# A decoder layer on one core: the hand-over between its parts, and w_out in blocks with sums

## The chip, the cores and the metric

One of the eight cores of a Trainium2 chip runs the whole kernel. The metric is the time in microseconds (us) that the device takes for one execution. TensorE does the matrix products and transposes, VectorE (DVE) and ScalarE (ACT) the arithmetic on tiles, GpSimd (POOL) some more of it; SyncE (SP) issues most DMAs.

## The reference

One layer for 256 tokens of 2048 features, in float32:

```
x = x + 1/2 * post1(SwiGLU_1(pre1(x)))             # FFN 1, 5632 hidden features
h = pre_mix(x);  q,k,v of two groups of 8 heads = h @ w_in
o_a = MoBA attention (one block of 256: causal softmax, partial rotary)
o_b = stick-breaking attention
x = x + post_mix(concat(norm_a(o_a), norm_b(o_b)) @ w_out)
x = x + 1/2 * post2(SwiGLU_2(pre2(x)))             # FFN 2
```

All `pre`, `post` and `norm` are RMS norms with a gain per feature. SwiGLU is `(silu(x @ w_gate) * (x @ w_up)) @ w_down`. All weights come from HBM once.

## The kernel before

**Precision.** A product of float32 is made of three matmuls on parts: every weight piece (128 x 1024 numbers) is split into a high part `whi` (a cast on ScalarE, L137) and a low part `wlo` (raw minus high, on VectorE, L142); so are the activations. The three terms are high x high, high x low, low x high. `Weights` keeps a list of pieces in the order of use, loads their blocks (up to 1 MB, three buffers, `RAW`) on SP's queue and splits three pieces ahead of the one in use (four buffers, `PARTS`). `get(i)` returns a split piece.

**Blocks with sums.** In most of the gate/up and down products, pairs of feature tiles are multiplied by the seven-product scheme for 2 x 2 blocks (two token tiles, two chunks of 512 columns): 21 matmuls instead of 24, for four sums of weights on VectorE (L104 to L110) and sums of results at the end (L913 to L924). A block holds eight PSUM banks, `1` to `7` and `X`. Plain pairs add into banks `2`, `3`, `4`, `X`. `w_out` has no such block: `products` runs it over chunks (0, 1), then 2, then 3, all plain.

**The end of a part.** The down product of an FFN ends with a tail: three pairs of feature tiles, over chunk 2 for both token tiles, then over chunk 3, token tile 0 first. From there on `ordered()` fixes the order of TensorE, VectorE, ScalarE and GpSimd as written. `handover` gives the end of the part: the last chunk of token tile 0, its RMS factor (`column`: nine small instructions of VectorE after the last sum of squares), updates of the residual `xn` (L696), the first transposes of the new `xn`; `take_over` goes on with the first three pieces of the next part, token tile by token tile, woven with the rest of the updates and transposes. GpSimd takes part: it splits halves of pieces (L142) and adds updates that ScalarE has scaled (L698, L699). The last part ends in `end_f2`, with the updates and the output DMAs.

**Small work** that need not stand at one place (`later`, `step`) is put in a list and taken up one entry a piece. SBUF beyond the weights is 30 slots of 4 KB a partition; who gives one back lets the next taker have it, in the order of giving.

Of the kernel before, what the change touches and what calls it, by code (L numbers as in the profile page):

```python
# [17 lines left out]
P = 128  # L18
# [42 lines left out]
class Weights:  # L61
# [5 lines left out]
    def __init__(self, nc, pool):  # L67
        self.nc, self.pool = nc, pool
        self.blocks, self.raw, self.pieces, self.parts = [], {}, [], {}
        self.loaded = self.split = 0  # L70

# [57 lines left out]
    def split_next(self):  # L129
# [5 lines left out]
        hi = self.pool.tile([P, nk, cols], F32R, tag="whi", name=f"whi{n}", bufs=self.PARTS)  # L135
        lo = self.pool.tile([P, nk, cols], F32R, tag="wlo", name=f"wlo{n}", bufs=self.PARTS)
# [4 lines left out]
        def low(eng, k0=0, k1=nk):  # L141
            eng.tensor_sub(lo[:, k0:k1], raw[:, k0:k1], hi[:, k0:k1].bitcast(F32))  # L142
            if then:
                then(self.raw[b])

        return low, lambda eng: low(eng, 0, nk // 2), lambda eng: low(eng, nk // 2, nk)

    def split_to(self, i):
        while self.split <= min(i, len(self.pieces) - 1):
            self.split_next()[0](self.nc.vector)  # L150
# [28 lines left out]

PLAIN = (("2", "3"), ("4", "X"))  # L180
# [9 lines left out]
H_SUMS = HALVES[0][1] + HALVES[1][1]  # L190


@with_exitstack
def hybrid_layer(ctx: ExitStack, tc: tile.TileContext, a):
# [56 lines left out]
    def plan_down(n, half, w):  # L251

        pairs, sums, tail = HALVES[half]
        for u in range(2):
            c0 = u * 2 * CH
            plan["down", n, half, u] = [
# [3 lines left out]
        if tail:  # L260
            for c in (2, 3):
                k = 2 * tail[0]
                plan["tail", n, c] = W.add(w, k, 4, c * CH, CH) + W.add(w, k + 4, 2, c * CH, CH)

    def plan_rows(w, ks):

        ks = list(ks)
        out = []
        for c0, cols in ((0, 2 * CH), (2 * CH, CH), (3 * CH, CH)):
            nk = 2048 // cols  # L270
            out.append([])
            for k in range(0, len(ks), nk):
                ids = W.add(w, ks[k], nk, c0, cols)
                out[-1] += [(k + m * nk // 2, i) for m, i in enumerate(ids)]
        return out
# [16 lines left out]
    def plan_mix():  # L292
        plan_v(1)
        plan_qk(1)
        plan_qk(0)
        plan_v(0)
        plan["o"] = plan_rows(a["w_out"], [g * NH + h for g in (1, 0) for h in range(NH)])
# [152 lines left out]
    class Pre:  # L450
# [12 lines left out]
        def update(self, c, t, eng=None):  # L463
            if self.post and (c, t) not in self.ready:
                self.post.update(c, t, eng)
# [71 lines left out]
    def product(name, pieces, x_of, done, cs, end=None):  # L537


        ps = [[bank(f"{name}_{t}{c}") for c in cs] for t in range(NT)]  # L540

        def mm(t, piece, part):
            k0 = piece[0]
            last = piece is pieces[-1]
            for j in range(part[2]):
                mm_tok(ps[t], part, j, x_of(k0 + j), t, k0 + j == 0, last and j == part[2] - 1)

        for piece in pieces[:-3] if end else pieces:
            part = W.get(piece[1])
            for t in range(NT):  # L550
                mm(t, piece, part)
            step()
        if end:
            held = [(piece, W.get(piece[1], 2 - m)) for m, piece in enumerate(pieces[-3:])]
            end([lambda t=t: done(t, cs[0], ps[t][0]) for t in range(NT)], lambda t, m: mm(t, *held[m]))
        else:
            for t in range(NT):
                for p, c in zip(ps[t], cs):
                    done(t, c, p)

    def products(name, groups, x_of, post, end):
        for m, cs in enumerate(((0, 1), (2,), (3,))):
            product(f"{name}{m}", groups[m], x_of, post.take, cs, end if m == 2 else None)

    def take_over(pre, mm, ids, need):

        after, los = pre.pending
        parts = [W.get(ids[m], 1 - m) for m in range(2)]
        if need == 4:
            his, los10 = pre.turn(1, (0,))  # L570
            run_all(his)
            _, low0, low1 = W.split_next()
            low1(nc.gpsimd)
            weave(after, los + los10)
            mm(0, parts[0], 0)
            pre.update(0, 1)
            low0(nc.vector)
        else:
            _, low0, low1 = W.split_next()
            low1(nc.gpsimd)  # L580
            weave(after[:6], los)
            mm(0, parts[0], 0)
            his, los10 = pre.turn(1, (0,))
            run_all(his)
            weave(after[6:], [lambda: low0(nc.vector)] + los10[:need])
        parts.append(W.get(ids[2], 0))
        pre.update(0, 1)
        pre.update(1, 1, nc.gpsimd)
        mm(1, parts[1], 0)
        if need == 2:  # L590
            mm(2, parts[2], 0)
            pre.post.finish(2)
        his, los = pre.turn(0, (1,))
        run_all(his)
        if need == 4:
            mm(2, parts[2], 0)
        run_all(los)
        run_all(los10[need:])
        mm(0, parts[0], 1)
        _, low0, low1 = W.split_next()  # L600
        pre.post.finish()
        low0(nc.vector)
# [757 lines left out]
```

## Time and profile before

| | us |
|---|---|
| time, median of 3 runs | 1873.37 (1873.2 to 1873.61) |
| the profiled execution, its time | 1873.02 |
| its span, first to last instruction | 1871.2 |
| TensorE matmuls busy | 1837.3 (98%) |
| VectorE busy | 1480.8 (79%) |
| ScalarE busy | 1012.3 (54%) |
| GpSimd busy | 115.4 (6%) |

The span is what the profile shows in detail; the time is the span and what lies around it. A busy TensorE can still run at half its clock, and its matmuls are drawn longer than the 0.23 us by which they follow each other. Idle time counts where the engine is needed next.

### The profile page before, as it was taken

Reading aid. Unit: us, or ns where it says so; the run is one execution under the profiler, and the core shown is the slowest. Engines: PE = TensorE matmul, PEld = TensorE weight load, DVE = VectorE, ACT = ScalarE, POOL = GpSimd, SP = SyncE. Lnnn points to the kernel's source line nnn. Section 1 sums busy time; section 2 is a strip of 40 time slices with the busy share of each in tenths; the row PEclk is TensorE's granted clock in tenths of the full one; section 3 lists DMA queues with packets and bytes.
Section 4 is the critical chain, followed back from the end, with each engine's and each line's share of the span. In section 5 each row is a group of like instructions: output and inputs, shape, how many; then the busy total and the mean of one; then the engine's idle time right before and its main releaser. Section 6 shows DMA issues by size and latency. Waiting matters only on the chain.

```text
span 1871.2 us, 23266 instructions
## 1 busy us (share of the span) xinstructions
PE 1837.3 (98%) x8638; PEld 1530.4 (82%) x8638; DVE 1480.8 (79%) x2026; ACT 1012.3 (54%) x1359; POOL 115.4 (6%) x117
## 2 busy tenths in 40 slices
PE   9999999999999998999999999999999999999997
PEld 8888888888888876888888887888888888888875
DVE  6987889778888888656786557888888778887887
ACT  7655555445555545655545446755555445555553
POOL 0000000000000002000353103000000000000001
PEclk9999999999999999999999999999999999999999
DMA  8555555455566654554445556455554555555643
GB/s 271 172 200 202 186 197 203 181 209 195 180 209 209 247 194 157 180 180 158 158 159 183 181 175 207 164 190 208 207 193 171 218 185 203 204 207 185 247 181 135
DMA packets 183121, 359.90 MB, mean 192 GB/s; under 512 B 8864, under 2 KB 58208, under 8 KB 183008
## 3 DMA queue, kind: packets, MB, share of 16 engines
q1 hardware_dynamic: 180624, 351.31, 53.8%
q0 software_dynamic: 2208, 7.04, 1.1%
q8 instruction: 68, 1.11, 0.2%
q14 instruction: 45, 0.37, 0.1%
q10 hardware_dynamic: 176, 0.07, 0.0%
HBM read 354.19 MB, written 4.19 MB: 192 GB/s over the span
## 4 chain that ended last, share of the span: by engine, by line
PE 91%; DVE 5%; ACT 1%; issue 1%; DMA 1%; POOL 0%; DVEq 0%; ACTq 0%; POOLq 0%
PE b L872 36%; PE d L872 19%; PE b_X L872 9%; PE pq L516 6%; PE pw L535 4%; PE pv L535 4%; PE d_X L872 4%; PE pq L525 3%; PE p L516 2%; DVE wlo L142 1%; PE p L525 1%; PE ht L952 1%; DVE xn L696 1%; ACT whi L137 1%; DMA raw<-in_ffn_w_gate_dram 0%
## 5 line engine op out<-in xcount | busy, mean ns | idle before, releaser
L137 ACT CAST whi<-raw 128x1024 fp32r<-128x1024 f32 (+1 forms) x793 | 790.9, 1014 | 735.4 <-PE b_X L872 301.0
L142 DVE TENSOR_TENSOR wlo<-raw,whi 128x1024 fp32r<-128x1024 f32 (+1 forms) x789 | 919.6, 1186 | 335.6 <-ACT whi L137 333.2
L872 PE MATMUL b<-whi,x 128*128 128x512 f32 x1440 | 443.9, 389 | 0.0
L872 PEld LDWEIGHTS b<-whi,x 128*128 128x128 f32 x1440 | 270.2, 188 | 56.3
L872 PE MATMUL b<-wlo,x 128*128 128x512 f32 x720 | 243.9, 389 | 0.7 <-DVE wlo L142 0.7
L872 PE MATMUL d<-whi,h 128*128 128x512 f32 x720 | 222.6, 389 | 0.4 <-ACT whi L137 0.4
L872 PE MATMUL b_X<-whi,x 128*128 128x512 f32 x480 | 186.9, 389 | 0.0
L872 PEld LDWEIGHTS b<-wlo,x 128*128 128x128 f32 x720 | 135.0, 188 | 29.6 <-DVE wlo L142 1.6
L872 PEld LDWEIGHTS d<-whi,h 128*128 128x128 f32 x720 | 135.0, 188 | 29.3 <-ACT whi L137 1.3
L516 PE MATMUL pq<-xg_mix,whi 128*128 128x512 f32 x512 | 131.8, 399 | 0.0
L872 PE MATMUL d<-wlo,h 128*128 128x512 f32 x360 | 122.5, 389 | 0.0
L516 PEld LDWEIGHTS pq<-xg_mix,whi 128*128 128x128 f32 x512 | 92.2, 189 | 16.9
L872 PEld LDWEIGHTS b_X<-whi,x 128*128 128x128 f32 x480 | 90.1, 188 | 19.0 <-issue 0.4
L872 PE MATMUL b_X<-wlo,x 128*128 128x512 f32 x240 | 93.4, 389 | 0.0
L872 PE MATMUL d_X<-whi,h 128*128 128x512 f32 x240 | 91.8, 389 | 0.0
L535 PE MATMUL pv<-whi,xg_mix 128*128 128x512 f32 x256 | 85.3, 405 | 1.7 <-ACT xg_mix L445 1.7
L872 PEld LDWEIGHTS d<-wlo,h 128*128 128x128 f32 x360 | 67.6, 188 | 14.1
L535 PE MATMUL pw<-whi,om 128*128 128x512 f32 x256 | 75.2, 391 | 0.0
L525 PEld LDWEIGHTS pq<-xg_mix,wlo 128*128 128x128 f32 x512 | 69.8, 190 | 5.3
L525 PE MATMUL pq<-xg_mix,wlo 128*128 128x256 f32 x512 | 71.3, 282 | 0.0
L535 PEld LDWEIGHTS pv<-whi,xg_mix 128*128 128x128 f32 x256 | 49.3, 193 | 12.6 <-ACT xg_mix L445 2.3
L516 PE MATMUL p<-xg_f,whi 128*128 128x512 f32 x224 | 58.1, 397 | 0.0
(300 smaller groups left out, 2440.9 us busy)
## 6 DMA issues: line engine op xcount, KB each, us to landing
raw<-in_ffn_w_down_dram SPq DMA_DIRECT2D x86, 1024.0 KB, 5.0
raw<-in_ffn_w_up_dram SPq DMA_DIRECT2D x168, 512.0 KB, 4.8
raw<-in_ffn_w_gate_dram SPq DMA_DIRECT2D x167, 512.0 KB, 3.8
raw<-in_w_in_dram SPq DMA_DIRECT2D x48, 1024.0 KB, 5.2
raw<-in_w_out_dram SPq DMA_DIRECT2D x16, 1024.0 KB, 5.0
raw<-in_ffn_w_gate_dram SPq DMA_DIRECT2D x4, 1024.0 KB, 6.7
raw<-in_ffn_w_up_dram SPq DMA_DIRECT2D x4, 1024.0 KB, 5.7
xn<-in_x_dram SPq DMA_DIRECT2D x8, 256.0 KB, 6.0
```

The costliest lines, as they stand in the source:

```text
L137: self.nc.scalar.copy(hi, raw)
L142: eng.tensor_sub(lo[:, k0:k1], raw[:, k0:k1], hi[:, k0:k1].bitcast(F32))
L516: nc.tensor.matmul(p, wh, x, start=k == 0, stop=False)
L525: nc.tensor.matmul(p[:, :T], lo[:, j, f * P:(f + 1) * P], xs(k)[:, 0, :], start=False, stop=k == KD - 1)
L535: nc.tensor.matmul(ps[c], y, w[:, j, c * CH:(c + 1) * CH], start=first and n == 0, stop=last and n == 2)
L696: nc.vector.scalar_tensor_tensor(x, f, self.z[t], x, op0=ALU.mult, op1=ALU.add)
L872: nc.tensor.matmul(self.ps[x], y, w, start=m == 1, stop=m == self.n[x])
L952: nc.tensor.transpose(p4[:, 2 * j + t], tg[2 * t + 1][:, k * P:(k + 1) * P], ident)
```

## The change

Six things are changed together.

- `w_out` becomes two blocks of two chunks (`Rows`, the old `Down` made general): eight pairs of feature tiles, two of them with sums (`OUT`). The heads' outputs for those pairs are turned into sums too (`put_om`).
- The tail of a part (`Rows.tail`) holds all six pieces: three for chunk 2 and three for chunk 3. Token tile 0 goes through both chunks, then token tile 1. `w_out` now has such a tail.
- Before the tail's first matmul, the next part's first four pieces (`AHEAD`) are split, into slots.
- `take_over` runs those four pieces for token tile 0, then for token tile 1.
- No arithmetic of the hand-over runs on GpSimd. The DMAs that keep `xn` for later stay in its queue.
- `end_f2` goes by token tile as well; all updates are VectorE's.

```diff
+AHEAD = 4
+OUT = ((4, 5, 6, 7, 0), (5, 7), (1, 2, 3))       # pairs, those with sums, the tail
...
-    def split_next(self):
+    def split_next(self, take=None):
...
-        hi = self.pool.tile([P, nk, cols], F32R, tag="whi", name=f"whi{n}", bufs=self.PARTS)
-        lo = self.pool.tile([P, nk, cols], F32R, tag="wlo", name=f"wlo{n}", bufs=self.PARTS)
+        hi, lo = (
+            take([P, nk, cols], F32R, f"{x}{n}") if take
+            else self.pool.tile([P, nk, cols], F32R, tag=x, name=f"{x}{n}", bufs=self.PARTS)
+            for x in ("whi", "wlo"))
...
+    def take_over(pre, mm, ids):
+        parts = [W.get(ids[m], 0) for m in range(AHEAD)]
+        for m in range(AHEAD):
+            mm(m, parts[m], 0)
+        W.split_next()()
+        his, los = pre.turn(0, (1,))
+        run_all(his)
+        run_all(los)
+        his, los = pre.turn(1, (1,))
+        run_all(his)
+        mm(0, parts[0], 1)
+        run_all(los)
+        pre.update(2, 1)
+        mm(1, parts[1], 1)
+        W.split_next()()
+        pre.update(3, 1)
+        mm(2, parts[2], 1)
+        pre.group(2)
+        mm(3, parts[3], 1)
...
     def handover(post, make):
+        def end(finish, mm):
             ordered()
+            for m in range(AHEAD):
+                W.split_next(slots.take)()
+            mm(0, 0)
+            finish(0, 0)
             before, after = post.column(0)
+            run_all(before)
+            mm(0, 1)
+            finish(1, 0)
+            post.finish()
+            run_all(after)
+            mm(1, 0)
             pre = make()
             pre.update(0, 0)
+            pre.update(1, 0)
+            his, los = pre.turn(0, (0,))
+            run_all(his)
+            finish(0, 1)
             before, after = post.column(1)
             run_all(before)
+            run_all(los)
+            his, los = pre.turn(1, (0,))
+            run_all(his)
+            run_all(los)
             mm(1, 1)
+            pre.update(2, 0)
+            pre.update(3, 0)
+            finish(1, 1)
+            post.finish()
+            run_all(after)
+            pre.update(0, 1)
+            pre.update(1, 1)
         return end
...
+    class Rows(Block):
...
+        def finish(self, c, t):
+            f = self.place(c, t)
+            self.join(f, c, t)
+            if self.last:
+                self.post.take(t, self.c[c], f)
+
+        def tail(self, end):
+            held = []
+            while todo:
+                step()
+            for m, (p, i) in enumerate(self.tail_pieces):
+                if m >= W.PARTS - 1:
+                    W.split_next(slots.take if m >= W.PARTS else None)()
+                held.append((self.xs[p], W.get(i, 0)))
+
+            def mm(t, c):
+                for x, part in held[3 * c:3 * c + 3]:
+                    for j in range(2):
+                        self.plain(x[:, j], part, j, t, (c,))
+
+            end(self.finish, mm)
...
-    products("pw", plan["o"], lambda k: om(order_o[k]), post, end_mix(post))
+    for u in range(2):
+        d = Rows(f"w{u}", ("o",), om, "o", OUT[1], post, u)
+        d.go()
+    d.tail(handover(post, next_pre("pre2", G[:, G_F2PRE:G_F2PRE + KD], "f2", post)))
...
     def end_f2(post):
+        def end(finish, mm):
             ordered()
+            for t in range(NT):
+                mm(t, 0)
+                finish(0, t)
+                before, after = post.column(t)
+                run_all(before)
+                mm(t, 1)
+                finish(1, t)
+                post.finish()
+                run_all(after)
+                for c in range(NC):
+                    put(post, c, t)
```

## Rows read from the trace of the kernel before

**Rows 1.** The page's part 1: busy us, share of the span, instructions.

```profile
PE 1837.3 (98%) x8638; PEld 1530.4 (82%) x8638; DVE 1480.8 (79%) x2026; ACT 1012.3 (54%) x1359; POOL 115.4 (6%) x117
```

**Rows 2.** Windows: length, busy us of PE, PEld, DVE, ACT, POOL, granted clock, DMA.

```profile
60.00:280.00 220.00, 219.66 (x987) 180.54 (x987) 183.91 (x233) 119.08 (x142) 0.55 (x1) 1.00 0.56 194
...
625.00:727.00 102.00, 101.11 (x447) 82.46 (x445) 88.44 (x112) 54.79 (x68) 4.12 (x7) 1.00 0.59 209
727.00:757.00 30.00, 22.59 (x92) 17.61 (x93) 25.85 (x48) 15.65 (x33) 12.69 (x7) 0.83 0.35 109
...
1040.00:1130.00 90.00, 90.00 (x407) 74.70 (x406) 49.83 (x79) 42.12 (x62) 5.07 (x6) 1.00 0.48 164
```

**Rows 3.** Timeline of TensorE at both joints: start, length, count [idle before].

```profile
730.51 1.12 PE L479 MATMUL xt_mix<-ident,xn 128*128 128x128 f32 x4 [3.55 <-DVE xn L696]
...
751.13 1.48 PE L535 MATMUL pv<-whi,xg_mix 128*128 128x512 f32 x3
...
1133.78 0.66 PE L479 MATMUL xt_f<-ident,xn 128*128 128x128 f32 x4 [2.74 <-DVE xn L696]
...
1152.05 2.02 PE L516 MATMUL p<-xg_f,whi 128*128 128x512 f32 x8
```

**Rows 4.** Windows at the joints, columns as in rows 2; the clock is third from last.

```profile
729.50:733.00 3.50, 1.12 (x4) 0.72 (x4) 2.58 (x8) 0.94 (x4) 0.00 (x0) 0.52 0.62 190
733.00:736.40 3.40, 3.31 (x9) 2.62 (x10) 2.75 (x13) 1.94 (x6) 1.38 (x1) 0.50 0.29 113
...
1135.90:1139.20 3.30, 3.28 (x14) 2.99 (x14) 3.30 (x12) 2.16 (x5) 1.76 (x2) 0.50 0.87 306
```

**Rows 5.** Timeline of TensorE, VectorE and SP's queue at the program's end.

```profile
1857.52 0.39 PE L872 MATMUL d_X<-whi,h 128*128 128x512 f32 x1
...
1857.80 1.41 DVE L696 SCALAR_TENSOR_TENSOR xn<-fg_f,rs_post_f,xn 128x512 f32<-128x512 f32 x2
...
1858.58 9.18 SPq L1300 DMA_DIRECT2D out_dram<-xn  x8
...
1859.39 0.68 DVE L924 TENSOR_TENSOR fg_f<-d_X,fg_f 128x512 f32<-128x512 f32 x1
...
1861.73 1.07 DVE L372 SCALAR_TENSOR_TENSOR rs_post_f<-rs_post_f 128x1 f32<-128x1 f32 x1
...
1863.84 3.08 DVE L696 SCALAR_TENSOR_TENSOR xn<-fg_f,rs_post_f,xn 128x512 f32<-128x512 f32 x3
```

**Rows 6.** The chain that ended last: start, length, matmuls of `w_out`.

```profile
1057.56 69.41 PE pw L535 x306
```

**Rows 7.** Groups by line and shape: count, busy us, mean ns of one, idle before.

```profile
L142 DVE TENSOR_TENSOR wlo<-raw,whi 128x1024 fp32r<-128x1024 f32 x713 | 863.5, 1231 | 335.4 <-ACT whi L137 333.0
L142 DVE TENSOR_TENSOR wlo<-raw,whi 128x512 fp32r<-128x512 f32 x76 | 57.9, 761 | 0.2 <-ACT whi L137 0.2
...
L137 ACT CAST whi<-raw 128x1024 fp32r<-128x1024 f32 x723 | 747.9, 1052 | 655.1 <-PE b_X L872 238.4 <-PE d_X L872 91.5 <-DVE raw L105 59.7
```

**Rows 8.** Timeline of VectorE at the first joint.

```profile
704.49 3.49 DVE L142 TENSOR_TENSOR wlo<-raw,whi 128x1024 fp32r<-128x1024 f32 x3
...
714.50 1.22 DVE L142 TENSOR_TENSOR wlo<-raw,whi 128x1024 fp32r<-128x1024 f32 x1
...
722.92 0.69 DVE L924 TENSOR_TENSOR fg_f<-d,fg_f 128x512 f32<-128x512 f32 x1 [1.65 <-PE d L872]
...
724.47 0.21 DVE L399 TENSOR_SCALAR rs_post_f<-ssq_post_f,rs_post_f 128x1 f32<-128x1 f32 x1 [0.60 <-ACT sqd L388]
...
727.00 2.61 DVE L142 TENSOR_TENSOR wlo<-raw,whi 128x512 fp32r<-128x512 f32 x1
...
744.71 4.18 DVE L696 SCALAR_TENSOR_TENSOR xn<-fg_f,rs_post_f,xn 128x512 f32<-128x512 f32 x2
```

**Rows 9.** DMA issues: count, size, median us from issue to landing.

```profile
raw<-in_ffn_w_gate_dram SPq DMA_DIRECT2D x167, 512.0 KB, 3.8
raw<-in_w_in_dram SPq DMA_DIRECT2D x48, 1024.0 KB, 5.2
```

More of the change, by code (lines that the diff above doesn't have):

```diff
@@ L251, in plan_down, with plan_rows @@
     def plan_down(n, half, w):
-        pairs, sums, tail = HALVES[half]
+        plan_rows(("down", n, half), w, *HALVES[half])
+    def plan_rows(key, w, pairs, sums, tail):
         for u in range(2):
             c0 = u * 2 * CH
-            plan["down", n, half, u] = [
+            plan[(*key, u)] = [
                 (p, W.add_sums(w, 2 * p, c0) if p in sums else W.add(w, 2 * p, 2, c0, 2 * CH))
@@ L260, in plan_down @@
         if tail:
+            plan[(*key, "tail")] = []
             for c in (2, 3):
                 k = 2 * tail[0]
[L263 to L275, printed above, removed]
+                ids = W.add(w, k, 4, c * CH, CH) + W.add(w, k + 4, 2, c * CH, CH)
+                plan[(*key, "tail")] += list(zip(tail, ids))
     def plan_v(g):
@@ L296, in plan_mix @@
         plan_v(0)
-        plan["o"] = plan_rows(a["w_out"], [g * NH + h for g in (1, 0) for h in range(NH)])
+        plan_rows(("o",), a["w_out"], *OUT)
     plan_ffn(1)
@@ L535, in mm_tok @@
                     nc.tensor.matmul(ps[c], y, w[:, j, c * CH:(c + 1) * CH], start=first and n == 0, stop=last and n == 2)
[L537 to L592, printed above, removed]
+    def take_over(pre, mm, ids):
[3 more added lines that the diff above has]
+        W.split_next()()
@@ L748, in first_pair @@
             if pre.post:
-                first = 3
-                take_over(pre, mm, [i for _, _, i in ids], 4)
+                first = AHEAD
+                take_over(pre, mm, [i for _, _, i in ids])
             else:
@@ L927, in ffn @@
-        waiting = []
         def gate_up_block(u):
@@ L1039, in ffn @@
             for u in range(2):
-                d = Down(half, u)
+                d = Rows(f"d{n}{half}{u}", ("down", n, half), hx, f"h{n}_", HALVES[half][1], post, u,
+                         more if half else None, half == 1)
                 d.go()
-                if (half, u) != (1, 1):
-                    for c, t in ((1, 0), (0, 0), (0, 1), (1, 1)):
-                        d.finish(c, t)
+        slots.give(*(f"more{n}{m}" for m in range(2)))
         d.tail(end_of(post))
-        slots.give(*(f"more{n}{m}" for m in range(2)), *(f"h{n}_{p}" for p in HALVES[1][2]), *post.rows.names)
+        slots.give(*post.rows.names)
         return post
```

346 lines of the change are left out of this document (138 added, 208 removed).

## The prediction

> **What bounds the kernel now.** I read the busy shares first: TensorE is busy 1837.3 us of 1871.2, VectorE 79%, GpSimd 6% [rows 1]. So only two things can move the time: fewer matmuls, or the 34 us in which TensorE does nothing, plus the time at half clock, which counts as busy. Next come the stages: in the gate/up blocks TensorE is full (219.66 of 220) while VectorE is at 84%; in the second down product it is nearly full at 87%; in `w_out` VectorE has room, 49.83 us of 90 [rows 2]. The holes are at the joints: in the 30 us after the first FFN's last matmul TensorE is busy 22.59 us, VectorE 25.85 and GpSimd 12.69 [rows 2]. The TensorE timeline shows what ends them: the first transposes of the next part start at 730.51, after a wait of 3.55 us for VectorE's update of `xn`; after `w_out` the wait is 2.74 us [rows 3]. Around them the granted clock falls to 0.50, that is 1.2 GHz [rows 4]; each us so spent costs half a us. Last, the end of the program: nothing but VectorE, ScalarE, GpSimd and the output DMAs after the last matmul [rows 5].
>
> **Two scales.** A matmul of 512 columns costs 69.41/306 = 0.227 us [rows 6], and a block with sums uses the same shape. I count each joint from S, the end of the last whole block ahead of the six tail pieces: the last matmul is drawn up to 730.51-3.55 = 726.96, 0.39 long; by its 0.227 it ends at 726.8, and 72 tail matmuls (16.33 us) before that put S at 710.49. For `w_out` the same gives 1133.78-2.74 = 1131.04, so 1130.87 and S = 1114.54; for the end of the program the last matmul starts at 1857.52, so S = 1841.42 [rows 3, 5]. The profiled execution took 1873.02 us, 0.35 under the median of the runs; the sums below are changes, so I add them to 1873.37.
>
> **w_out by blocks.** Before: 16 feature tiles x 4 chunks x 2 token tiles x 3 terms = 384 matmuls. After: twelve plain pair-products of 24 and four with sums of 21, 372. That removes 12 x 0.227 = 2.7 us of TensorE work. It adds to VectorE: four sums of weights for each of the four sum pairs, 16 x 0.69 = 11.0 (a join of that size, 128x512, takes 0.69); 1.5 more pieces each, 6 x 1.16 = 7.0 (three in a row take 3.49, so one each 1.16, [rows 8]); the joining of the banks, 16 x 0.68 = 10.9. So 49.8 + 28.9 = 78.7 us of 87, 90%. The two stages at 84% and 87% lose 0.3 us in 220 and 0.9 in 102 [rows 2]. A sum pair alone asks VectorE for 3.5 x 1.16 + 4 x 0.69 = 6.8 us against 4.76 of TensorE, short by 2.0; a plain pair gives back 5.44 - 2.32 = 3.1, and pieces are split only three ahead. So between nothing and 4 x 2.0 = 8.0; I take 1.3, nearer to the stages at similar load. Net -1.4.
>
> **No GpSimd arithmetic.** A split of 128x512 has taken 0.76 on average; at 727.00, while GpSimd splits its own piece, 2.61, and two updates at 744.71 take 4.18 where two take 1.41 at 1857.80 [rows 5, 7, 8]. These two places alone lose 1.85 + 2.77 = 4.6 us of VectorE in one joint. What it takes over there from GpSimd's eight instructions is 2 x 1.16 + 3 x 0.69 for splits, and three updates of 0.7 whole: 6.5 us. So VectorE's total in a joint changes by little (+1.9 by these rows, less by others that are stretched), and its order in the queue decides. The Trainium skill (Perfetto Trace Analysis, Optimizing Scalar/DVE Operations) says that work may be offloaded from a saturated VectorE, even to GpSimd, and adds that it may not help as the two share a port; by the first half alone each joint would pay the 6.5 us, 9.2 more in all than by these rows (1882), and the stretched instructions do not bear that out; the second half they do.
>
> **First joint, step by step.** New code puts into VectorE's and ScalarE's in-order queues, ahead of `finish(0, 0)`, the last tail splits and four splits of the next part. All must be over before the chain to the new `xn` starts. Loads decide when: with three raw buffers, the second block of `w_in` (pieces three and four of those four) can only load when the split of tail piece five of six has freed its buffer. In the old trace that split ends at 714.50+1.22 = S+5.2 [rows 8]; it waits for the same load and buffers in the new order (S+4.0 if the sums' adds come behind it). A block of `w_in` lands 5.2 us after its issue [rows 9]: S+10.4, say 10.5. Two casts of 1.05 and the second's split of 1.2 behind them [rows 7]: the queue is free at S+14.0 (12.5 to 14.6). Then the chain: join 0.69, square to its sum 0.8, two small 0.35, second join to its sum 1.55 (722.92 to 724.47, [rows 8]), nine small ones 2.0, update 0.7: 6.2. Transposes at S+20.2, as before (20.02). But TensorE has then done only 54 of its 72 matmuls, to S+12.25, and idles 8.0 us. After it: transposes of two chunks, the second 0.7 behind, at half clock, to 22.0; 18 matmuls 4.1; half clock for 3.4 us or twice that (it lasted from about 729.6 to 736.4 in the first joint and 3.4 in the second, [rows 4]), costing 1.7 to 3.4, I take 2.0: 28.1. Four pieces for token tile 0, 24 x 0.227 = 5.4: 33.5. By then VectorE has updated tile 1 (join at 28.1, +1.55+2.0+0.7 = 32.4). Eight transposes and the first cast 0.9, 24 matmuls 5.4, eight more transposes 0.9: 40.8 and 0.2 of small waits, 41.0. Before, the 48th such matmul ends at 751.55+0.43 = S+41.5 [rows 3]. So -0.5 (bounds: -3.0 where the queue is free at 12.5 and the clock recovers early; +1.5).
>
> **Second joint.** The next part's pieces are blocks of 512 KB, one each, so three buffers make a chain: the fourth can load only when the first is split. Such a block lands after 3.8 [rows 9], and the first is asked for at S; VectorE, which has the two last joins (1.2), three tail splits and this one, ends it at 6.3; the fourth block lands at 6.3 + 3.8 = 10.1, cast 1.05, split 1.2: free at 12.45 (11.9 to 13.5). Chain 6.2: transposes at 18.65 against 1133.78 = S+19.24 before [rows 3], with 18 matmuls fewer done. Idle 6.4 us against 2.74. Then 20.2 after the transposes; 18 matmuls with half clock, 4.1 + 2.0: 26.3; four pieces by token tile, 32 x 0.12 = 3.9: 30.2; update of tile 1 at 26.5 + 4.3 = 30.8; transposes, the split queued ahead and the first low part to 33.1, a hole of 1.9 after the transposes that had cover before; 64 x 0.12 + 0.9 = 8.6: 41.7. Before, the fifth piece starts at 1152.05 = S+37.5 [rows 3]. So +4.2 (bounds +1.5 and +5.5): here nothing waited for three loads in a row before.
>
> **The end.** No next part, so VectorE's queue is free in time. Before, the last join starts at 1859.39, 1.4 after the last matmul's end, since updates of tile 0 stand ahead of it; one small instruction takes 1.07 instead of 0.16; the last three updates 3.08 where three of 0.7 are 2.1, and a fourth runs on GpSimd; the last two outputs are issued 0.4 apart up to 1867.4 [rows 5]. After: last matmul S+16.33 = 1857.8, join at 1858.0, +1.55+2.0, four updates 2.8: 1864.35, last issue then. That is 3.0 earlier (2.3 to 3.4). The updates of tile 0 cost nothing: their chain starts at S+8.3 and, 6.3 long, ends at S+14.6, under the last 18 matmuls, which run to S+16.33; each us by which they overran would make the last join as much later.
>
> **Sum:** -1.4 -0.5 +4.2 -3.0 = -0.7, so 1872.7 us. An edge of 0.2% (3.7 us) is about what a measurement of this kernel can tell.
>
> **Rivals.** *First, faster: the splits ahead are no hindrance.* If the next loads land before VectorE comes to them, its own work sets the queue: the first joint is free at 6.3 + 4 x 1.16 = 10.9 instead of 14.0, the second at 9.7 instead of 12.45. That is -5.8, or 1866.9. If the splits were off the chain altogether, the join would start at S+4.3, the transposes follow mm(0,1) at 12.6, and both joints lose nearly no clock: -18, 1855. For it: VectorE is idle much of S+7 to S+12 now. Against: buffer count and the landing times of [rows 9]. It decides from a queue free before S+11. 0.28.
> *Second, slower: VectorE becomes the bound of `w_out`.* Place: the sum pairs, 2.0 us short each, in u = 0 also with the scaling of `om` (about 0.9 a head) in the same queue. Price: if nothing is made up, 8.0 instead of 1.3, +6.0, 1879.4; it decides from 5.7 us lost there. For it: 90% is above all that the trace shows with a full TensorE. Against: VectorE idles ahead of it. 0.20. The rule of the page named above comes out on this side too, by another way (VectorE's 6.5 us in each joint, 1882 us); the stretched instructions speak against it, and 0.02 of the 0.20 is its.
> *Third, my forecast*, the gains of end and matmuls eaten in the second joint: 0.52.
>
> **Chances and range.** Forecast 0.52: 0.46 within 0.2%, 0.03 on each side. First rival 0.28, faster. Second 0.20: 0.18 slower, 0.02 within. So faster 0.31, same 0.48, slower 0.21. The forecast's own bounds: ends of the single terms, not all at once, -5 to +4 us, 1868.4 to 1877.4. The range takes in the nearer form of the first rival and most of the second: 1866 to 1878.5, leaving out 0.2 (rival one's far form and rival two's worst).
>
> **What would show it.** Right: transposes of `xt_mix` and `xt_f` some 8 and 6 us after the 54th tail matmul; the split of the fourth next piece immediately ahead of the first join in VectorE's order, waiting for its cast, and that for a load; half clock in both joints; no GpSimd arithmetic there and splits of 1.2; the span's end some 13.4 - 3.0 = 10.4 us after the last matmul. Wrong: a first join at S+4 to S+8; holes of over 1 us in `w_out` at matmuls that wait for `wlo`; a tail at the end as long as before. A step that would break the sum most is the time at which VectorE's queue is free: each us there is one us in each joint.

## The result, and the profile after

The changed kernel takes 1883.72 us (median of four, 1881.92 to 1884.4) against 1873.28 (1872.83 to 1873.61) for the kernel before on the same chip: ratio 1.0055, 95% interval 1.0039 to 1.0071. It is 10.4 us slower; I had forecast 1872.7 and a range of 1866 to 1878.5. The profiled executions differ by 11.35 us of span (1871.20 and 1882.55), which I read here; that of the changed kernel is the slowest of its four.

The page's part 1, to be held against [rows 1]:

```profile
PE 1835.2 (97%) x8634; PEld 1528.5 (81%) x8634; DVE 1502.7 (80%) x2087; ACT 1013.3 (54%) x1358; POOL 83.5 (4%) x96
```

TensorE is busy 2.1 us less; the time went into holes. What TensorE waited for (line that waited, releaser: total us, times, longest):

```profile
PE xt_f L480 <- DVE xn L649: 12.0, 2, 10.9
PE xt_mix L480 <- DVE xn L649: 10.5, 1, 10.5
PE sp L1135 <- POOL qk L1106: 4.5, 1, 4.5
...
PE ss_a L423 <- POOL acc_a L416: 1.1, 1, 1.1
```

In the kernel before, the waits for `xn` in front of the first transposes were 2.74 us long for `xt_f` and 3.55 for `xt_mix` [rows 3]. To place the rest I cut the span at starts of matmuls on TensorE's timeline: the 54th tail matmul of FFN 1 (the last one ahead of the transposes; before, the last matmul minus 18 x 0.227), the first of the projection of q and k, the first of `w_out`, its 54th tail matmul, the last that spreads FFN 2's row factors (`pr_f`), the program's last matmul, the end. The first two lines are these two kernels, the others the experiments below (profiled executions, us):

| kernel | to 54th | joint 1 | attention | w_out | joint 2 | FFN 2 | end | span |
|---|---|---|---|---|---|---|---|---|
| before | 722.5 | 64.7 | 252.9 | 86.4 | 45.9 | 685.1 | 13.7 | 1871.2 |
| changed | 721.5 | 64.7 | 256.6 | 86.9 | 55.7 | 685.0 | 12.2 | 1882.5 |
| splits behind | 721.6 | 65.2 | 256.0 | 87.2 | 51.0 | 685.0 | 12.2 | 1878.2 |
| the same, two on GpSimd | 722.7 | 64.7 | 255.1 | 86.9 | 51.9 | 685.0 | 12.2 | 1878.6 |
| w_out plain | 721.7 | 64.8 | 252.9 | 86.4 | 52.9 | 685.1 | 12.2 | 1876.0 |
| scaling later | 721.8 | 66.1 | 253.5 | 86.9 | 53.5 | 685.1 | 12.2 | 1879.1 |
| loads early, joint 2 | 721.8 | 67.1 | 255.3 | 89.5 | 45.2 | 685.0 | 11.9 | 1875.7 |
| loads early, both | 725.3 | 55.1 | 255.7 | 89.2 | 45.4 | 685.1 | 12.0 | 1867.9 |
| loads early, same order | 721.6 | 60.7 | 255.5 | 86.9 | 49.0 | 685.1 | 12.1 | 1870.7 |
| loads early, splits behind | 722.3 | 63.9 | 255.4 | 86.9 | 49.7 | 685.1 | 12.0 | 1875.4 |
| end reordered | 722.6 | 66.7 | 255.5 | 87.6 | 54.0 | 685.1 | 10.9 | 1882.4 |
| best | 726.5 | 55.1 | 252.7 | 86.4 | 44.9 | 685.1 | 10.8 | 1861.5 |

So +9.8 in the second joint, +3.7 in the attention, +0.5 in `w_out`, nothing in the first joint, -1.5 at the end, -1.0 ahead of it all.

Other lines show how far these differences hold, where they have the same work in a column. The second joint takes 52.9 to 55.7 us with the same splits and loads (w_out plain, scaling later, end reordered), the attention 255.1 to 256.6 with its sums at the same place (all lines but before, w_out plain, scaling later and best), the first joint 64.7 to 67.1 where it is left as it was (those three of the second joint, and loads early, joint 2). So the second joint costs 7.0 to 9.8, the attention 2.2 to 3.7 and the first joint 0 to 2.4; the changed kernel's own line has an end of each.

**The joints.** VectorE's timeline (start, length, count [idle before]), first joint and then second:

```profile
722.80 2.36 DVE L147 TENSOR_TENSOR wlo<-raw,whi 128x1024 fp32r<-128x1024 f32 x2 [2.92 <-ACT whi L142]
725.08 0.68 DVE L744 TENSOR_TENSOR fg_f<-d,fg_f 128x512 f32<-128x512 f32 x1
...
1123.23 1.23 DVE L147 TENSOR_TENSOR wlo<-raw,whi 128x1024 fp32r<-128x1024 f32 x1 [0.84 <-ACT whi L142]
1125.89 1.23 DVE L147 TENSOR_TENSOR wlo<-raw,whi 128x1024 fp32r<-128x1024 f32 x1 [1.44 <-ACT whi L142]
1128.30 1.23 DVE L147 TENSOR_TENSOR wlo<-raw,whi 128x1024 fp32r<-128x1024 f32 x1 [1.18 <-ACT whi L142]
1132.46 1.23 DVE L147 TENSOR_TENSOR wlo<-raw,whi 128x1024 fp32r<-128x1024 f32 x1 [2.94 <-ACT whi L142]
1133.60 0.68 DVE L744 TENSOR_TENSOR fg_mix<-w,fg_mix 128x512 f32<-128x512 f32 x1
1135.08 0.69 DVE L654 TENSOR_TENSOR fg_mix<-fg_mix,r_mix_post_g 128x512 f32<-128x512 f32 x1 [0.79 <-ACT sqd L389]
...
1138.08 0.21 DVE L400 TENSOR_SCALAR rs_post_mix<-ssq_post_mix,rs_post_mix 128x1 f32<-128x1 f32 x1
...
1140.08 1.41 DVE L649 SCALAR_TENSOR_TENSOR xn<-fg_mix,rs_post_mix,xn 128x512 f32<-128x512 f32 x2
```

The four splits of next pieces, each waiting for its cast, and right behind the fourth the first join: the order is as foreseen. ScalarE's timeline says what the casts wait for, SP's queue when the fourth load was issued:

```profile
721.73 1.99 ACT L142 CAST whi<-raw 128x1024 fp32r<-128x1024 f32 x2 [3.29 <-DMA raw<-in_w_in_dram]
...
1131.38 1.04 ACT L142 CAST whi<-raw 128x1024 fp32r<-128x1024 f32 x1 [3.17 <-DMA raw<-in_ffn_w_up_dram]
```

```profile
1124.48 0.37 SPq L126 DMA_DIRECT2D raw<-in_ffn_w_up_dram  x1
```

It was issued when the first split (1123.23+1.23) had freed a buffer and used 6.9 us later. S, the start of the six tail pieces, is the 54th matmul's end minus 54 x 0.227: 709.5 and 1117.6 by TensorE's timeline:

```profile
721.51 0.39 PE L692 MATMUL d<-whi,h 128*128 128x512 f32 x1
732.37 1.97 PE L480 MATMUL xt_mix<-ident,xn 128*128 128x128 f32 x8 [10.47 <-DVE xn L649]
...
951.32 0.80 PE L1135 MATMUL sp<-qk 128*128 128x128 f32 x2 [4.47 <-POOL qk L1106]
...
1129.65 0.39 PE L692 MATMUL w<-whi,o 128*128 128x512 f32 x1
1140.89 1.97 PE L480 MATMUL xt_f<-ident,xn 128*128 128x128 f32 x8 [10.85 <-DVE xn L649]
...
1870.35 0.39 PE L692 MATMUL d_X<-whi,h 128*128 128x512 f32 x1
```

First joins at S+15.6 and S+16.0, transposes at S+22.9 and S+23.3, holes of 10.5 and 10.9 us. The windows (columns as in [rows 2]) show the clock at each hole, in the attention too:

```profile
712.00:725.00 13.00, 9.90 (x44) 7.83 (x42) 8.40 (x8) 4.79 (x5) 0.54 (x1) 1.00 0.91 325
725.00:735.20 10.20, 2.83 (x11) 2.64 (x12) 6.95 (x20) 3.55 (x12) 0.00 (x0) 0.50 0.35 118
...
940.00:950.30 10.30, 6.85 (x42) 5.93 (x40) 10.30 (x19) 5.14 (x8) 4.42 (x4) 1.00 0.31 102
950.30:957.00 6.70, 5.68 (x16) 4.73 (x17) 4.34 (x12) 0.58 (x1) 4.18 (x5) 0.50 0.47 157
...
1134.60:1144.80 10.20, 3.91 (x14) 3.43 (x15) 7.22 (x23) 3.95 (x14) 1.13 (x2) 0.50 0.30 104
...
1155.00:1158.50 3.50, 3.45 (x16) 3.45 (x17) 3.50 (x9) 1.57 (x4) 0.54 (x1) 0.51 0.72 225
```

**The attention.** From 940.0 to 950.3 VectorE has no gap at all (10.30 of 10.30; before, 9.89 of 10.00 from 940 to 950, so a full queue is not new, but the sums in it are). GpSimd, which rotates the heads, waits 5.80 us for VectorE's shuffle and then needs 4.1 us itself (4.00 and 2.6 at the same place before); its last step releases TensorE at 951.32:

```profile
947.16 0.92 POOL L1104 TENSOR_TENSOR sh<-sh,rots 32x256 f32<-32x256 f32 x1 [5.80 <-DVE sh L1103]
948.05 2.36 POOL L1105 TENSOR_TENSOR qk<-qk,rots 32x256 f32<-32x256 f32 x1
950.48 0.78 POOL L1106 TENSOR_TENSOR qk<-qk,sh 32x256 f32<-32x256 f32 x1
```

In the kernel before there are two such waits, shorter ones, at full clock:

```profile
PE sp L1173 <- POOL qk L1144: 3.2, 2, 1.8
```

So TensorE waits only 1.3 us more in all; the rest of the loss is the stretch at half clock, where it is busy for 5.68 us.

**The end.** VectorE's timeline, to be held against [rows 5]:

```profile
1867.03 2.74 DVE L649 SCALAR_TENSOR_TENSOR xn<-fg_f,rs_post_f,xn 128x512 f32<-128x512 f32 x4
1869.69 0.68 DVE L744 TENSOR_TENSOR fg_f<-d,fg_f 128x512 f32<-128x512 f32 x1
...
1872.08 0.68 DVE L744 TENSOR_TENSOR fg_f<-d_X,fg_f 128x512 f32<-128x512 f32 x1
...
1874.22 0.21 DVE L400 TENSOR_SCALAR rs_post_f<-ssq_post_f,rs_post_f 128x1 f32<-128x1 f32 x1
```

The four updates of tile 0 end at 1869.77, and the join of tile 1's third chunk, whose matmuls were over, stands behind them with its product and sum. So the last join starts 1.7 us after the start of the last matmul.

### The profile page after: what moved, and what is told of

It is laid out like the page before. It is cut to its first block, busy times and chain, and to the rows that moved or that the text cites. A ratio compares the mean times of both kernels' runs of the same rounds, so it can differ in the third digit from the quotient of the medians.

```text
span 1882.5 us, 23279 instructions
## 1 busy us (share of the span) xinstructions
PE 1835.2 (97%) x8634; PEld 1528.5 (81%) x8634; DVE 1502.7 (80%) x2087; ACT 1013.3 (54%) x1358; POOL 83.5 (4%) x96
## 3 DMA queue, kind: packets, MB, share of 16 engines
q1 hardware_dynamic: 179360, 351.31, 53.5%
## 4 chain that ended last, share of the span: by engine, by line
PE 88%; DVE 8%; ACT 2%; DMA 1%; issue 1%; POOL 0%; DVEq 0%; SPq 0%; ACTq 0%; POOLq 0%
PE b L692 36%; PE d L692 17%; PE b_X L692 9%; PE pq L517 5%; PE pv L536 4%; PE d_X L692 4%; DVE wlo L147 3%; PE pq L526 3%; PE p L517 3%; PE w L692 2%; PE p L526 2%; ACT whi L142 1%; PE ht L951 1%; PE w_X L692 1%; ACT sqd L389 1%
## 5 line engine op out<-in xcount | busy, mean ns | idle before, releaser
L692 PE MATMUL b<-whi,x_1h 128*128 128x512 f32 x140 | 55.1, 424 | 0.3 <-ACT whi L142 0.3
## 6 DMA issues: line engine op xcount, KB each, us to landing
xn<-in_x_dram SPq DMA_DIRECT2D x8, 256.0 KB, 6.1
```

Source lines behind the costliest of these rows:

```text
L692: nc.tensor.matmul(self.ps[x], y, w, start=m == 1, stop=m == self.n[x])
```

## The experiments

Theory: the joints have their holes because the four splits stand in VectorE's in-order queue ahead of the chain to the new `xn` and wait there for loads that go through three buffers. Rivals: the order of the queue alone does it; VectorE's volume of work does it whatever the order; the loads alone do it. Line numbers of experiments are shifted by the added lines. Each is held against the kernel before on the same chip, whose medians were 1873.23 (1 to 4), 1872.99 (5, 8, 9, 10) and 1872.86 (6, 7).

### 1. The splits behind the chain

```diff
-            for m in range(AHEAD):
-                W.split_next(slots.take)()
             mm(0, 0)
             finish(0, 0)
             before, after = post.column(0)
             run_all(before)
+            W.split_next(slots.take)()
...
             run_all(his)
+            W.split_next(slots.take)()
             finish(0, 1)
...
             mm(1, 1)
+            for m in range(2):
+                W.split_next(slots.take)()
```

> The four splits of next pieces are no longer ahead of the chain: one stands behind the small operations of tile 0, one behind the transposes' casts, two behind the last tail matmuls. Nothing else is changed. Changed kernel, profiled: S = 709.49 and 1117.63, first joins at S+15.6 and S+16.0, transposes at 732.37 and 1140.89 after idle 10.5 and 10.9 us. Theory (VectorE's in-order queue, held by the four splits, makes both holes): first join at S+5 to S+7, transposes at S+12.5 to S+14 in both joints, holes under 1.5 us, the half clock gone or half as long; 8 to 10 us less in each joint than the changed kernel has, part of it given back where pieces three and four are late for token tile 0 (up to 3 us each): 1866 to 1871 us. Rival (the loads of the next pieces bound the joint however the splits are queued): transposes early, but TensorE then waits for the fourth piece until about S+15 or later and works at half clock anyway; under 5 us gained, over 1878 us.

Measured: 1878.67 us, ratio 1.0029 (1.0017 to 1.0041). The transposes of tile 0 do come early (724.31, after a wait of 2.4 instead of 10.5), but the first joint gains nothing: 65.2. VectorE's timeline shows where the hole went:

```profile
731.64 2.15 DVE L447 SCALAR_TENSOR_TENSOR xg_mix<-xt_mix,G,xg_mix 128x128 fp32r<-128x128 f32 x8
733.71 2.35 DVE L147 TENSOR_TENSOR wlo<-raw,whi 128x1024 fp32r<-128x1024 f32 x2
735.98 1.41 DVE L651 SCALAR_TENSOR_TENSOR xn<-fg_f,rs_post_f,xn 128x512 f32<-128x512 f32 x2
737.30 0.68 DVE L746 TENSOR_TENSOR fg_f<-d_X,fg_f 128x512 f32<-128x512 f32 x1
```

The last join of tile 1 starts 6.3 us after the end of its last matmul (730.76+0.23), behind low parts, two splits and two updates. TensorE's timeline:

```profile
742.25 1.11 PE L480 MATMUL xt_mix<-ident,xn 128*128 128x128 f32 x4 [4.44 <-DVE xn L651]
```

The time is in the rival's range (over 1878), but what I had named for it is not what held TensorE: it waited for tile 1's `xn`, not for the fourth piece. The first hole is shrunk as the theory says, and a second of 4.4 us and two stretches at half clock (724 to 728, 742 to 748) take its place. In the first joint, what the order gains for tile 0, tile 1 loses; the second joint keeps a gain, 51.0 instead of 55.7, with a hole of 6.0 at tile 1.

### 2. w_out plain

```diff
-OUT = ((4, 5, 6, 7, 0), (5, 7), (1, 2, 3))
+OUT = ((4, 5, 6, 7, 0), (), (1, 2, 3))
...
-            nc.vector.tensor_add(x, self.ps[PLAIN[t][c]], x)
+            if self.sums:
+                nc.vector.tensor_add(x, self.ps[PLAIN[t][c]], x)
+            else:
+                nc.vector.tensor_copy(x, self.ps[PLAIN[t][c]])
```

> w_out without sums in the changed kernel: all pairs plain, twelve more matmuls of 512 columns, none of the four-operation sums in VectorE, neither on the weights nor on the attention outputs; the joints stay as they are. Theory (the sums of the attention outputs, put into VectorE's queue while GpSimd rotates the heads, make the 4.6 us wait for rope at 946.57 and the half clock behind it): the attention stage from its first projection matmul to the first matmul of w_out goes from 256.6 back to about 252.9 us; w_out gains its 3.0 us of stalls and loses 2.7 us of matmuls: 1879 to 1881 us in all. Rival (the wait for rope has another cause, such as the order in which slots come free): attention stays at 256 to 257 us, 1883 to 1884 us.

Measured: 1878.49, ratio 1.0028 (1.0018 to 1.0038), 0.5 below the range I gave. Attention 252.9 as before, with the two short waits of before:

```profile
PE sp L1138 <- POOL qk L1109: 3.2, 2, 1.8
```

`w_out` takes 86.4 with twelve matmuls more, 0.5 less than with sums: its 2.7 us of matmuls were worth less than the holes that the sums made. Part of the total is the second joint, 2.8 shorter: here the fourth load was issued at 1119.87 and used at 1124.49, after 4.6 us instead of 6.9:

```profile
1119.87 0.37 SPq L126 DMA_DIRECT2D raw<-in_ffn_w_up_dram  x1
```

```profile
1124.49 1.05 ACT L142 CAST whi<-raw 128x1024 fp32r<-128x1024 f32 x1 [1.33 <-DMA raw<-in_ffn_w_up_dram]
```

The edit does not touch these loads; experiments 3 and 9, with the same joint, have 4.7 and 5.1.

### 3. The scaling later

```diff
-    norm(1, 9)
+    norm(1, 28)
```

> The scaling of the first eight heads' outputs (with the sums of two pairs of them) starts 19 steps later, in the projection of v, where GpSimd rotates nothing. w_out keeps its sums. Theory (VectorE's extra work while GpSimd rotates heads makes the wait for rope): no wait over 2.5 us for rope, no half clock around 950, attention 252 to 254 us; -2.5 to -4 us: 1879.5 to 1881.5 us. Rival (another cause of that wait): unchanged, 1883 to 1884.5 us.

Measured: 1881.59, ratio 1.0051 (1.0037 to 1.0065), 0.1 over the range I gave. Its runs scatter (1880.09 to 1886.89), so the total tells little. The trace tells: the waits for rope are short again, and the attention takes 253.5:

```profile
PE sp L1135 <- POOL qk L1106: 3.3, 2, 1.7
```

With the same sums, moved off the rotations, 3.1 of the 3.7 us come back (at least 1.6, by the 255.1 of experiment 8), and the granted clock stays at 1.00 from 940 to 960.

### 4. Loads early, second joint

```diff
+    def early(self, take, i, n):
+        for b in range(i, i + n):
+            srcs, nk, cols, step = self.blocks[b]
+            t = take([P, nk, cols * len(srcs)], F32, f"early{b}")
+            for m, src in enumerate(srcs):
+                self.nc.gpsimd.dma_start(t[:, :, m * cols:(m + 1) * cols], src)
+            self.raw[b] = t
...
+            if self.tail_pieces and self.last and self.names == "o":
+                W.early(slots.take, W.pieces[self.tail_pieces[-1][1]][0] + 1, AHEAD)
             self.run(waiting, steps, lambda p: self.u and give(self.xs[p], self.names + str(p)))
```

> Second joint only: the four next pieces' loads go to buffers of their own and are asked for when the second half of w_out begins, on another DMA queue; the splits stay ahead of the chain, in the same order. The first joint stays as in the changed kernel. Theory (of those 16.0 us to the first join some 5 are a wait for loads that go through three buffers, the rest VectorE's own splits): first join at S+10 to S+11.5, transposes at S+17 to S+18.5 instead of S+23.3, hole of 5 to 6 us instead of 10.9, 4 to 7 us less in all: 1877 to 1880 us. Rival (the loads are not what the queue waits for): first join stays at S+15 or later, no gain; the order of the splits alone would then decide.

Measured: 1875.64, ratio 1.0014 (1.0005 to 1.0023): more than expected. The scheduler that orders the code outside the joints put loads and splits far ahead (the loads at 864 to 954; of the splits, two at 1107.13 and 1109.08, the last at 1121.83), so that only the tail's own three splits stood before the chain: first join 1127.96, S+6.3, hole 1.2. The joint takes 45.2, less than in the kernel before. In the first joint, left as it was, the second block of `w_in` was cast at 724.05 instead of 721.73, and the joint took 67.1 instead of 64.7: it follows the landing of that load.

### 5. Loads early, both joints

The same call in FFN 1's last block, and the first two blocks of `w_in` as four of 512 KB.

> As in the run with early loads, now at both joints: each joint's four next pieces (in the first joint loaded as four blocks of 512 KB instead of two of 1 MB) have buffers of their own and are asked for as the second half of the block before begins. In the second joint the splits then ran ahead of the joint altogether (first join at S+6.6, hole 1.3 us, 45.2 us from the 54th tail matmul to the spread of the row factors against 55.7 in the changed kernel). Theory (in the first joint too, the loads through three buffers hold VectorE's queue, and without them the chain of tile 0 starts as soon as tail piece six is split): first join at S+6 to S+7, transposes at S+12.5 to S+13.5, hole under 2 us, 67 to 71 us from S to the first projection of q and k instead of 76.7: 1867 to 1871 us. Rival (in the first joint VectorE's total work is the bound, as the run with the splits behind showed no gain there): early transposes, but tile 1's come as late as before, 74 us or more, and 1874 to 1877 us.

Measured: 1869.73, ratio 0.9983 (0.9974 to 0.9992). The theory holds: first join 719.62 = S+6.3 (S = 713.3), and of 10.5 us of wait 1.8 are left in the first joint:

```profile
719.62 0.68 DVE L760 TENSOR_TENSOR fg_f<-d,fg_f 128x512 f32<-128x512 f32 x1
...
PE xt_mix L495 <- DVE xn L665: 1.8, 2, 1.2
```

It has a price ahead: FFN 1's last block reaches its 54th tail matmul 3.8 us later, and `w_out` takes 89.2. Early splits, not early loads, have this price: experiment 6, with the loads alone early, has 721.6 and 86.9. That they do it by loading VectorE where sums are taken fits experiment 10 (no sums in `w_out`, 86.4) but is not shown for FFN 1.

### 6. Only the loads away

```diff
         def tail(self, end):
...
+            ordered()                       # was the first line of end()
```

On top of experiment 5. This fixes the order from the tail on, so the four splits stay between the tail's splits and the chain, as in the changed kernel; their loads have landed long before.

> The changed kernel's order in VectorE's queue at both joints (three tail splits, four next splits, then the chain of tile 0), but the four next pieces' loads have long landed in buffers of their own; unlike in the run with early loads at both joints, the four splits can't run ahead of the joint. So the loads alone are taken away, and VectorE's work in the joint is what it is in the changed kernel. Theory (the loads hold the queue for some 5 us, the work of the four splits for another 4.6): first joins at S+10.5 to S+11.5 in both joints (changed kernel S+15.6 and S+16.0; splits ahead of the joint S+6.3), transposes at S+17 to S+18, holes of 5 to 6 us, each joint 3 to 5 us less than in the changed kernel: 1874 to 1878 us. Rival A (only the loads matter): 1868 to 1871, as with splits ahead. Rival B (only the splits' work matters): no gain, over 1881.

Measured: 1873.01, ratio 1.0001 (0.9992 to 1.0010), between the theory's range and that of rival A. The joins decide, and neither rival fits them (A: S+6.3, B: no gain). VectorE's timeline in the first joint:

```profile
712.39 3.49 DVE L160 TENSOR_TENSOR wlo<-raw,whi 128x1024 fp32r<-128x1024 f32 x3
715.80 4.63 DVE L160 TENSOR_TENSOR wlo<-early,whi 128x1024 fp32r<-128x1024 f32 x4
720.34 0.69 DVE L759 TENSOR_TENSOR fg_f<-d,fg_f 128x512 f32<-128x512 f32 x1
```

Seven splits without a gap, the join at S+10.8 (second joint 1122.35, S+9.8), holes of 5.7 and 4.7 us. So of the 15.6 and 16.0 us, 4.8 and 6.2 were waits for loads, 4.6 the splits' own time, the rest mostly the tail's.

### 7. Early loads, splits behind

Experiments 5 and 1 together.

> Early loads at both joints as in the run before, and the splits put behind the chain as in the first experiment (1878.7 us there, with late loads). VectorE then has the same work between S and tile 1's transposes as in that experiment, but no load to wait for. Theory (there VectorE's work bound tile 1, not the loads): tile 1's transposes still about S+32 in the first joint, 76 to 77 us from S to the first projection of q and k; in the second joint, where piece four landed late, 1 to 4 us less: 1874 to 1878 us. Rival (the loads bound it there too): 67 to 70 us, 1867 to 1871 us in all, as with splits ahead of the joint.

Measured: 1878.70, ratio 1.0031 (1.0019 to 1.0044), as slow as with late loads and above the range I gave. Joint 1 63.9 (65.2 with late loads), joint 2 49.7 (51.0). Behind the chain, the loads hardly matter: there the order and the amount of work hold tile 1. The second split still waits 1.98 us, for a cast that ScalarE makes behind the high parts of the new transposes, and tile 1's first join, whose matmuls ended at 722.5, stands behind that split at 728.79. Experiment 1 has a like wait there (2.23 us).

### 8. Two splits on GpSimd

```diff
-                W.split_next(slots.take)()
+                W.split_next(slots.take)(nc.gpsimd)     # in experiment 1, pieces three and four
```

> The run with the splits behind the chain (1878.7 us), but the low parts of pieces three and four are taken by GpSimd. In that run VectorE worked without a gap from 728.3 to 746 in the first joint, 2.4 us of it these two splits, and TensorE waited 4.4 us for tile 1's update. Theory A (VectorE's total work in the joint is the bound, and GpSimd takes some of it off): tile 1's transposes 1 to 2.4 us earlier in each joint: 1874 to 1877 us. Theory B (GpSimd's work stretches VectorE's at the same time, as a 128x512 split of 2.61 instead of 0.76 us did in the kernel before): GpSimd needs over 4 us for each split, the update of tile 1 comes no earlier or later, and the four pieces wait for GpSimd's part: 1878 to 1883 us.

Measured: 1880.91, ratio 1.0043 (1.0030 to 1.0055): in theory B's range. VectorE's timeline, then GpSimd's:

```profile
731.58 2.15 DVE L447 SCALAR_TENSOR_TENSOR xg_mix<-xt_mix,G,xg_mix 128x128 fp32r<-128x128 f32 x8
733.65 4.79 DVE L651 SCALAR_TENSOR_TENSOR xn<-fg_f,rs_post_f,xn 128x512 f32<-128x512 f32 x2
```

```profile
732.74 5.16 POOL L147 TENSOR_TENSOR wlo<-raw,whi 128x1024 fp32r<-128x1024 f32 x2 [3.73 <-ACT whi L142]
```

GpSimd takes 2.35 us of splits off VectorE, needs 5.16 for them (less than the 4 each that B named), and the two updates beside them take 4.79 instead of 1.41. Nothing is won: joints 64.7 and 51.9 against 65.2 and 51.0. The Trainium skill (SBUF — State Buffer, Who interferes with whom) says that a VectorE instruction with two inputs in SBUF contends with a GpSimd instruction that reads SBUF, and that one with at most one SBUF input doesn't (outside VectorE's two-port modes). The trace agrees: the updates read both inputs from SBUF and are stretched, those low parts that run beside the same splits (L447 from 732.74 on) read one from PSUM and keep 0.27 us each.

### 9. The end reordered

```diff
+                if t == 1:
+                    put(post, 0, 0)
+                    put(post, 1, 0)
+                    post.gap = [lambda: put(post, 2, 0)]   # between a join and its product
                 finish(0, t)
...
                 finish(1, t)
+                if t == 1:
+                    put(post, 3, 0)
```

> Only the end of the program is changed: one update of tile 0 stands between the join of tile 1's third chunk and its product with the gain, one behind the very last join, where VectorE waits for ScalarE's square; the others stay ahead. Changed kernel: last matmul starts at 1870.35, last join at 1872.08, span ends 12.20 after that matmul. Theory (VectorE's queue with tile 0's updates and the work of the third chunk holds the last join by 1.3 us): last join at 0.3 to 0.6 after the last matmul's start, span end 10.7 to 11.2 after it; time lower by about 1.2 us, at the edge of what the runs can tell. Rival (the outputs' transfers set the end): join earlier, end the same 12.2.

Measured: 1881.48, ratio 1.0046 (1.0032 to 1.0060). VectorE's timeline; the last matmul starts at 1871.55:

```profile
1869.53 0.68 DVE L746 TENSOR_TENSOR fg_f<-d,fg_f 128x512 f32<-128x512 f32 x1
1870.13 0.74 DVE L649 SCALAR_TENSOR_TENSOR xn<-fg_f,rs_post_f,xn 128x512 f32<-128x512 f32 x1
...
1871.97 0.69 DVE L746 TENSOR_TENSOR fg_f<-d_X,fg_f 128x512 f32<-128x512 f32 x1
```

The last join stands 0.42 after the last matmul's start and the span ends 10.9 after it, 1.3 less: the queue, not the transfers, held it. The total, 2.2 under the changed kernel's, is within the scatter of both and shows nothing by itself.

### 10. The parts together

Experiments 5, 2 and 9.

> Early loads at both joints, w_out with plain pairs alone, and at the end of the program two updates of tile 0 moved into VectorE's waits (one behind the last join but one, one behind the last join). If the parts add: the run with early loads at both joints, less 3.7 us of attention, less 0.5 us of w_out, less 1.3 us at the end, so 5 us under it: 1862 to 1866 us. If they don't add (the joints then gain less since loads collide with other traffic): over 1867.

Measured: 1863.21 (1860.47 to 1863.31), ratio 0.9943 (0.9930 to 0.9955): the parts add, and this beats both kernels, 10 us under the one before. With plain pairs `w_out` keeps its 86.4 even with the early splits in it.

## Why the prediction was wrong

The sum said -0.7 and the span says +11.35; -1.0 of that lies ahead of the joints, where the runs themselves scatter by 1.2 (721.5 to 722.7 where nothing there was changed).

**Second joint, +4.2 forecast, +9.8 measured: the step that failed most.** The mechanism was as written, and the queue order line for line; the size was wrong. I gave the fourth load 3.8 us, the median of the blocks of `w_gate` [rows 9]; but the fourth block is one of `w_up`, and the same page of the kernel before gives those a longer median:

```profile
raw<-in_ffn_w_up_dram SPq DMA_DIRECT2D x168, 512.0 KB, 4.8
```

In the profiled execution it took 6.9. The queue was free at S+16.0 instead of 12.45, beyond my bound of 13.5. The chain then took 7.3 us from join to transposes instead of 6.2, since I left out the two products with the gain (L654), which stand in the same queue: 1135.08 and the one ahead of L400. Together 4.6; the remaining 1.0 lies behind the transposes, where a second stretch at half clock (1155.0 to 1158.5) was not in the sum. Of this the 6.9 is the part that varies: in experiments 2, 3 and 9, with loads of 4.6 to 5.1, the queue was free at S+13.0 to S+13.8, the chain again took 7.3, and the joint was 7.0 to 8.1 longer than before. So the load and the queue were there close to my bound, and the joint was still 2.8 to 3.9 us worse than forecast. Experiment 6 prices the loads in this joint at 3.9 to 6.7 us (52.9 to 55.7 against 49.0), and experiments 4 and 5 the splits' own time in it at some 4 more.

**First joint, -0.5 forecast, 0.0 measured (up to +2.4 in the experiments that leave it as it was): near the forecast by luck.** The join came at S+15.6, beyond my bound of 14.6, the chain took 7.3 here too, and the transposes came 2.7 later than I said. But TensorE then ran on without a hole, at full clock from 735.2, and ended the 48th projection matmul (it starts at 751.51) 19.4 after the transposes' start where I had 20.8. By that mark, mine, the joint is 0.8 longer than before (S+42.3 against S+41.5) and not 0.5 shorter; up to the projection of q and k this is made good, as in the kernel before the clock was still low behind the mark (0.57 from 749.6 to 753.4, 1.00 now). The block of `w_in` was used 7 us after its issue (median 5.2): in this stretch, 712 to 725, the DMA engines were 91% busy and moved 325 GB/s, so that the traffic set the landing is likely, not shown. The Trainium skill (DMA: Bandwidth & Descriptors, Specifications) puts the HBM limit per core at about 358 GB/s, half of what the stack gives to two cores. This case's trace goes above it (386 GB/s from 738 to 740 in experiment 1), so that limit is not what held the load. In the second joint it was 207 GB/s between 1121 and 1134; why the fourth load took 6.9 there is not settled.

**Attention, 0 forecast, +3.7 measured: a step that was missing.** My sum has no term for the sums of the heads' outputs (`put_om`), though the change names them: it adds up the sums of weights, the pieces and the joining of banks, and the second rival names only the scaling of `om`, in `w_out`'s queue. The sums of the first eight heads stand in the stage before, while GpSimd rotates heads and TensorE waits for each. Experiments 2 and 3 show it twice, by taking the sums away (252.9) and by moving them (253.5).

**w_out, -1.4 forecast, +0.5 measured.** The 2.7 us of matmuls are gone and 3.2 of stalls came, not 1.3: within the bound of 8, but on the wrong side of even. 1.1 of them is a wait for GpSimd's sum of squares, 0.8 for casts; the rest I have only as matmuls that follow each other late in the second half's sums. VectorE didn't become the bound as rival two had it (3.2 against the 5.7 from which it decides); it was busy for 73.1 us of 88 there (1042 to 1130), where I had added up 78.7 of 87.

**The end, -3.0 forecast, -1.5 measured.** I had named one condition, that tile 0's updates overrun the last matmuls, which run to S+16.33. They were late (to 1869.77, S+15.5 instead of 14.6) but did not. Behind them stood the join, product and sum of tile 1's third chunk, which I had left out, and with those the last join came 1.2 us later than forecast. The product with the gain was missing here too, 0.6. Experiment 9 takes 1.3 back.

**No GpSimd arithmetic: right.** Splits in the joints take 1.23 us, none is stretched, and experiment 8 shows that GpSimd's help costs as much as it gives.

**The first rival.** Its condition, loads that land in time, did not hold in the changed kernel. Where experiment 6 makes it hold, its near form has the queue right: the join comes at S+10.8 and S+9.8, where I had 10.9 and 9.7. Its far form is wrong: "splits off the chain", for which I named 1855, gives 1878.7 with and without early loads, as much of the work only moves to tile 1. What gains is to have the loads early (1873.0) and then to do the splits before the joint as well (1869.7).

**Slips in the sums.** In the first joint the listed terms give a queue free at S+13.8, not 14.0, and a chain of 6.1, not 6.2. Before the change the last join came 1.6 us after the last matmul's end, not 1.4. Rival two's price is +6.7, as its 1879.4 has it, not +6.0. None of them changes the outcome.

## What to carry to other kernels

Work put ahead "for later" into an in-order queue costs the chain behind it its own time (here 4.6 us), and the wait for its data on top (here about as much again): count the loads it needs, with the landing times of a crowded stretch and not a median, and everything that stands behind it. Before moving it behind the critical chain, look at who is next in that queue: in the first joint the order moved a hole from one token tile to the other, and only taking the loads, and then the work, out of the stretch shrank it. A saving on a full engine has to be set against every queue in which its preparation stands, including those of the stage before.

## What the runs showed of the hardware

From within the holes of 10.5 and 10.9 us on, TensorE's granted clock was 0.50, that is 1.2 GHz, for about 10 us (725.0 to 735.2, 1134.6 to 1144.8), most of it still idle; with the 5.7 us hole of experiment 6 it was 0.66 on average over 725 to 735; with the holes of at most 1.2 us in experiment 5's first joint it was 1.00 from 713.1 to 749.1. So part of a hole is paid again behind it: TensorE is busy at half clock for 2.8 and 3.9 us in those two stretches, which costs about half of that (1.4 and 2.0 us, an estimate), and in the attention for 5.68 us, more than behind either of the longer holes.

The second block of `w_in` was cast 12.3, 12.4, 12.6, 13.0 and 14.3 us after the first one's issue (changed kernel, experiments 2, 3, 9 and 4; 709.46 to 721.73 in the first of them, 709.73 to 724.05 in the last), though nothing differs up to there, and the first joint took 64.7, 64.8, 66.1, 66.7 and 67.1: where a joint hangs on a landing, its time scatters with it.

Beside two splits of 128x1024 on GpSimd (5.16 us), two 128x512 updates of VectorE with both inputs in SBUF took 4.79 us instead of 1.41, while low parts with one input in PSUM kept their 0.27 each (experiment 8).
